# A hybrid encoder block: within-chunk products by array quadrants with compact operands, and two places for reloaded mixer outputs

## The chip, the cores and the metric

The kernel runs on one core of one Trainium2 chip. TensorE (PE) multiplies; VectorE (DVE), ScalarE (ACT) and GpSimd (POOL) do the rest; SyncE (SP) issues most of the transfers (DMA). The metric is the device time of one execution in microseconds (us), lower is better.

## The reference

One layer on 1024 tokens of width 1024: a projection, three parallel mixers (cross-attention to a memory, a Conformer convolution, a two-way RWKV-7 scan of 6 heads of 64), the output projection with its residual, then 16 experts that each pick 128 tokens. The part that the change touches is the scan and the output projection:

```python
def step(state, inp):
    r_t, w_t, k_t, v_t, kk_t, a_t = inp
    sa = jnp.einsum('bhij,bhj->bhi', state, -kk_t)
    state = (state * w_t[..., None, :]
             + sa[..., :, None] * (kk_t * a_t)[..., None, :]
             + v_t[..., :, None] * k_t[..., None, :])
    y_t = jnp.einsum('bhij,bhj->bhi', state, r_t)
    return state, y_t
...
x = x + jnp.concatenate([o_att, o_conv, o_rwkv], axis=-1) @ w_out[l]
x = x + expert_choice_ffn(rms_norm(x, norm_ffn_g[l]), w_router[l], w_e_gate[l], w_e_up[l], w_e_down[l])
```

## The kernel before

**Stages.** The projections, attention and convolution run first (to about 290 us of the trace), the scan follows (290 to about 750 us, overlapping the last projections at its start), then the rest of the output projection and the router, and from 890 us on the experts. Only the scan stage contains code that the change touches.

**The scan.** Sequences are cut into chunks of 64 tokens (`C`). Work is done in six units: three pairs of heads (one head on partitions 0 to 63, `lo`, the other on 64 to 127, `hi`) times two halves of the sequence; each unit holds 8 chunks (`HC`) for each of the two directions `d`. For one unit, `prep` builds two operands on DVE, ACT and POOL: `AR` (decayed kk and r, two blocks of 64 columns a chunk) and `BK` (k and b with the inverse decay, two blocks of 64). `within` multiplies them chunk by chunk into the within-chunk matrices; `prep2` transposes `BK` and v; `invert` solves a triangular system in 31 dependent steps on DVE (L910, L911); `chain` walks the 8 chunks one after the other, each a sequence of small products and copies: psX, Xs, psSA, SV, psS, S.

**The products of `within` before.** `BK` has room for both heads side by side, `[P, HC, 2, 2, C]`: the block that belongs to the other head is filled with zeros once (L668, L669), so that a product over all 128 partitions gives one head's result. A unit has four groups (a quarter of chunks `q`, a direction `d`), each with two tiles `psA`, one a head. A tile takes four matmuls of 128 rows by 128 columns with a moving operand of 128 columns, and is then multiplied by a mask into `AM` on DVE (L857). `psA` has two buffers in PSUM, so a tile is filled while the one before it is masked. ACT then copies parts of `AM` for `invert` (L895).

**The residual.** `residual` works off the first 5 of 8 row blocks of the output projection in 32 steps (4 column blocks of 256, 8 token blocks of 128). The mixer outputs were stored in DRAM as a high and a low part (`oT_d`) and are loaded back for each step as two tiles `fo`; 15 matmuls follow; DVE adds x (`fx`, L1089), and the sum goes to DRAM (L1090).

```python
1081                o = [Z["fw"].tile([P, 5, P], F32R, name=f"fo{j}", bufs=FOB) for j in range(2)]
1082                for j in range(2):
1083                    nc.sync.dma_start(o[j].bitcast(F32), oT_d[j][0:5, :, tok].rearrange("k p t -> p k t"))
1087                for k in range(5):
1088                    mm3(ps, o[0][:, k], o[1][:, k], wh[:, k], wl[:, k], k == 0, k == 4)
1089                V.tensor_add(xt, ps, xt)
```

With `FOB = 1` each of the two `fo` tiles has one place: the load of step i+1 must wait until the matmuls of step i have read it.

**What sets the order.** The stages are Python generators. `run` steps the `mains` in turn and puts steps of the `fills` (the next units' `prep`, `within`, `invert`, `prep2`, and the residual) between them by the numbers `R_*`. A scheduling layer then fixes the order on each engine; on the chip each engine, and SP's queue of transfers, works off its list in that order, and an instruction that waits holds up what stands behind it.

**Reading matmuls.** A matmul of 32-bit floats (`F32`) appears as two MATMUL records in the trace, so the eight matmuls of a pair of `psA` tiles are 16 records. Those of the residual and the projections are of another type (`F32R`) and appear as one.

Of the kernel before, what the change touches and what calls it, by code (L numbers as in the profile page):

```python
# [46 lines left out]
    _n += _w  # L47
NPC = _n

FOB = 1  # L50
RW = 1
LB = 1
KB = 2
# [47 lines left out]
def hybrid_block_kernel(ctx: ExitStack, tc: tile.TileContext, x, xT, memT, memn, w_in, w_mk, w_mv, pcols,  # L101
# [552 lines left out]
    def early():  # L654

        ph1r.close()
        Z["se"] = pool("se", bufs=2, stack=ph2r, side="right")
        Z["pcs"] = [Z["se"].tile([P, 2, HC], F32, name=f"pcs{i}", bufs=1) for i in range(3)]
        Z["s1"] = pool("s1", bufs=2, stack=ph2e, side="right")
        Z["ew"] = pool("ew", bufs=1, stack=ph2e, side="right")  # L660
        ge = pool("ge", stack=ph2e, side="right")
        Z["AR"] = [ge.tile([P, 2, HC, 2, C], F32, name="AR0")]
        Z["AM"] = [ge.tile([P, 4, 2, 2, C], F32, name=f"AM{i}") for i in range(4)]
        Z["TT"] = [ge.tile([P, NCH, 2, 32], F32, name="TT0")]

        Z["BK"] = [ge.tile([P, HC, 2, 2, C], F32, name=f"BK{d}") for d in range(2)]
        for bk in Z["BK"]:
            G.memset(bk[hi, :, 0], 0.0)  # L668
            G.memset(bk[lo, :, 1], 0.0)  # L669
        Z["ep"] = ge.tile([P, HC, C + 1], F32, name="ep")  # L670
        G.memset(Z["ep"][:, :, 0:1], 1.0)
        Z["dinit"] = dinit = ge.tile([P, 16, 32], F32, name="dinit")
        G.iota(dinit, pattern=[[-2, 16], [1, 32]], base=0, channel_multiplier=0,
               allow_small_or_imprecise_dtypes=True)
        V.tensor_scalar(dinit, dinit, lpar1, None, op0=ALU.is_equal)

        rst = ge.tile([P, HC, C], F32, name="rst")
        V.memset(rst, 1.0)
        V.memset(rst[:, :, 0:1], 0.0)
        Z["rst"] = rst.rearrange("p a b -> p (a b)")  # L680
        yield
# [93 lines left out]
    def prep(p, k, g):  # L775
        pd = pair[p]
        AR = g["AR"] = Z["AR"][g["u"] % 3]
        pcs = g["pcs"] = Z["pcs"][g["u"] % 3]
        if k == 0:
            pd["bonus"] = Z["se"].tile([P, NT, 2], F32, name="bonus", bufs=3)  # L780
            pd["prod"] = Z["s1"].tile([P, S], F32, name="prods", bufs=1)
        ins = [(load(f"k{p}", n), load(f"r{p}", n)) for n in (k, 1 - k)]
        for d in range(2):
            n = k if d == 0 else 1 - k
            rows = slice(d * 64, d * 64 + 64)
            kt, rt_ = ins[d]
            pw = mm()
            T.matmul(pw, lhsT=upw[rows, 0, p * P:(p + 1) * P], rhs=shifted["wd"][rows, half(k)], start=True, stop=True)
            pa = mm()
            T.matmul(pa, lhsT=upw[rows, 1, p * P:(p + 1) * P], rhs=shifted["ad"][rows, half(k)], start=True, stop=True)  # L790
            sg = Z["ew"].tile([P, HC, C], F32, name="sg", bufs=1)
            sg2 = sg.rearrange("p a b -> p (a b)")
            A.activation(sg2, pw, AF.Tanh, scale=0.5, bias=w0h[:, d * 3 + p:d * 3 + p + 1])
            ta = Z["ew"].tile([P, HC, C], F32, name="ta", bufs=1)
            A.activation(ta.rearrange("p a b -> p (a b)"), pa, AF.Tanh, scale=0.5,
                         bias=a0h[:, d * 3 + p:d * 3 + p + 1])
            yield
            if FL[0]:
                A.activation(sg2, sg2, AF.Identity, bias=1.0)
            else:  # L800
                V.tensor_scalar(sg, sg, 1.0, None, op0=ALU.add)
            cl = Z["ew"].tile([P, HC, C], F32, name="cl", bufs=1)
            V.tensor_tensor_scan(out=cl.rearrange("p a b -> p (a b)"), data0=Z["rst"], data1=sg2, initial=0.0,
                                 op0=ALU.mult, op1=ALU.add)
            ep = Z["ep"]
            A.activation(ep[:, :, 1:C + 1], cl, AF.Exp, scale=-0.5 * DECAY)

            A.activation(cl, cl, AF.Exp, scale=0.5 * DECAY)
            A.copy(pcs[:, d], ep[:, :, C])
            yield  # L810
            kk3, k3, r3 = chunks(pd["kk"][:, half(n)], d), chunks(kt, d), chunks(rt_, d)

            V.scalar_tensor_tensor(sg, ta, 1.0, kk3, op0=ALU.add, op1=ALU.mult)
            A.activation(ta, ta, AF.Identity, scale=kah[:, p:p + 1], bias=kac[:, p:p + 1])
            V.tensor_mul(AR[:, d, :, 0, :], kk3, ep[:, :, 0:C])
            yield
            (V, G)[FL[1]].tensor_mul(AR[:, d, :, 1, :], r3, ep[:, :, 1:C + 1])
            kd = ta
            (V, G)[FL[6]].tensor_mul(kd, k3, ta)
            yield  # L820

            BK = g["BK", d] = Z["BK"][d]
            V.tensor_mul(BK[lo, :, 0, 0, :], kd[lo], cl[lo])
            (G, V)[FL[7]].tensor_mul(BK[hi, :, 1, 1, :], kd[hi], cl[hi])
            for r_, h, i in ((lo, 0, 1), (hi, 1, 0)):
                V.scalar_tensor_tensor(BK[r_, :, h, i, :], sg[r_], -0.5, cl[r_], op0=ALU.mult, op1=ALU.mult)
            yield
            both = chunks(pd["prod"][:, half(n)], d)
            if k == 0:
                G.tensor_mul(both, kd, r3)  # L830
            else:
                prod = Z["ew"].tile([P, HC, C], F32, name="prod", bufs=1)
                G.tensor_mul(prod, kd, r3)
                G.tensor_add(both, both, prod)
            yield
        yield
# [8 lines left out]
    def within(g):  # L845

        for q, d in ((0, 0), (0, 1), (1, 0), (1, 1)):
            AM = g["AM", d, q] = Z["AM"][g["u"] % 2 * 4 + q * 2 + d]
            for h in range(2):
                ps = mm("A", shape=[P, 4, 2, C], name="psA", bufs=2)  # L850
                r_ = slice(h * 64, h * 64 + 64)
                for c in range(4):
                    cc = q * 4 + c
                    T.matmul(ps[:, c].rearrange("p a b -> p (a b)"),  # L854
                             lhsT=g["BK", d][:, cc, h].rearrange("p a b -> p (a b)"),
                             rhs=g["AR"][:, d, cc].rearrange("p a b -> p (a b)"), start=True, stop=True)
                V.tensor_tensor(AM[:, :, h], ps, mask[:, None].to_broadcast([P, 4, 2, C]), op=ALU.mult)  # L857
                yield

    def prep2(p, k, g):  # L860
        BT = g["BT"] = Z["BT"][g["u"] % 2]
        SV = g["SV"] = Z["SV"][g["u"] % 2]
        for d in range(2):
            n = k if d == 0 else 1 - k

            for h in range(2):
                ps = mm(shape=[P, HC, C])
                r_ = slice(h * 64, h * 64 + 64)
                for cc in range(HC):
                    T.transpose(ps[:, cc, :], g["BK", d][r_, cc, h].rearrange("p a b -> p (a b)"), ident[r_, r_])  # L870
                A.copy(BT[:, d, :, h, :], ps)
                yield

# [766 lines left out]
```

## Time and profile before

| | |
|---|---|
| three runs | 1480.89, 1490.68, 1491.66 us; median 1490.68 |
| the profiled execution | 1489.13 us, its span 1487.2 us |
| busy in the span | PE 90%, DVE 82%, ACT 56%, POOL 18% |
| granted clock of TensorE, mean of the span | 0.927 of 2.4 GHz |
| chain that ended last | PE 60%, DVE 23%, DMA 6%, ACT 5%, issue 4% |

Busy shares are averages over stages with different limits. The chain is followed back from the last instruction to whatever released each step; a time on it is a time on which the end depended in this execution. It does not tell how much slack the second-latest input had. Idle time in front of an instruction is given with what ended it.

### The profile page before, as it was taken

The page shows a single profiled execution, that of the slowest core. Times are in us where ns is not written, and L with a number is a line of the kernel's source. Part 1 is how long each engine was busy: PE and PEld are TensorE (multiplying, and loading weights), DVE is VectorE, ACT ScalarE, POOL GpSimd, SP SyncE. Part 2 cuts the span into 40 slices and gives each one's busy share as a digit, 9 for nine tenths or more (in the row PEclk, how much of TensorE's full clock was granted, in tenths as well). Part 3 has the DMA queues.
Part 4 walks back from the last instruction along what each step waited for, and adds up shares of the span by engine and source line. Part 5 has one row for each costly group of instructions (what it writes and reads, how often), then busy time and mean ns, then how long its engine had stood idle before and what let it go on. Part 6 is the DMA issues. An engine that isn't in the chain of part 4 may idle for free.

```text
span 1487.2 us, 24329 instructions
## 1 busy us (share of the span) xinstructions
PE 1333.4 (90%) x9238; PEld 1069.4 (72%) x9238; DVE 1216.1 (82%) x2120; ACT 831.2 (56%) x1214; POOL 266.4 (18%) x238
## 2 busy tenths in 40 slices
PE   6888999997888889888999719999999999999996
PEld 5777667675777776767868618888888887887773
DVE  8899975699686869696833678999999988998886
ACT  4222574433535244434322418888888877887875
POOL 2233322532120312130221000100000110110010
PEclk9999899998898888888999859999999999999998
DMA  8212112422443533342473657999999999999985
GB/s 294 71 61 67 64 64 97 152 71 73 141 143 93 157 97 117 105 121 84 142 272 142 269 198 293 386 393 390 385 385 390 381 379 344 370 377 377 370 302 201
DMA packets 146100, 327.91 MB, mean 220 GB/s; under 512 B 9792, under 2 KB 64960, under 8 KB 145984
## 3 DMA queue, kind: packets, MB, share of 16 engines
q1 hardware_dynamic: 139360, 303.14, 55.6%
q0 software_dynamic: 6192, 22.55, 5.4%
q8 instruction: 72, 1.18, 0.3%
q10 hardware_dynamic: 432, 0.68, 0.1%
q14 instruction: 44, 0.36, 0.1%
HBM read 288.58 MB, written 37.75 MB: 219 GB/s over the span
## 4 chain that ended last, share of the span: by engine, by line
PE 60%; DVE 23%; DMA 6%; ACT 5%; issue 4%; POOL 1%; SPq 0%; POOLq 0%; DVEq 0%; ACTq 0%
PE mm L330 14%; PE mm L331 14%; PE mm L329 14%; DVE cv L517 3%; DVE dtmp L910 2%; DVE Dt L911 2%; DMA fo<-oT_d 2%; PE mm L1435 2%; ACT Ld L895 2%; DMA xk<-in_xT_dram 1%; PE mm L745 1%; PE psA L854 1%; DVE ewl L1354 1%; PE mm L1165 1%; PE mm L1575 1%
## 5 line engine op out<-in xcount | busy, mean ns | idle before, releaser
L1354 DVE SCALAR_TENSOR_TENSOR ewl<-eraw,pc,ewh 128x1024 fp32r<-128x1024 f32 x256 | 315.6, 1280 | 30.5 <-ACT ewh L1353 28.4
L1353 ACT ACTIVATE ewh<-eraw,pc 128x1024 fp32r<-128x1024 f32 x256 | 283.8, 1149 | 31.7 <-PE mm L331 25.7
L330 PE MATMUL mm<-ewl,xh 128*128 128x512 f32 x512 | 202.1, 395 | 3.2 <-DVE ewl L1354 3.0
L331 PE MATMUL mm<-ewh,xl 128*128 128x512 f32 x512 | 200.1, 391 | 0.0
L329 PE MATMUL mm<-ewh,xh 128*128 128x512 f32 x512 | 190.4, 397 | 2.5 <-ACT ewh L1353 2.5
L1350 DVE TENSOR_TENSOR ewl<-eraw,ewh 128x1024 fp32r<-128x1024 f32 x120 | 139.0, 1219 | 2.8 <-ACT ewh L1349 2.8
L329 PE MATMUL mm<-hh,wh 128*128 128x512 f32 x304 | 125.4, 413 | 9.6 <-ACT hh L310 9.6
L1349 ACT ACTIVATE ewh<-eraw 128x1024 fp32r<-128x1024 f32 x120 | 121.6, 1057 | 10.6 <-PE mm L331 9.5
L331 PE MATMUL mm<-hh,wl 128*128 128x512 f32 x304 | 125.5, 413 | 0.8 <-POOL wl L325 0.8
L330 PE MATMUL mm<-hl,wh 128*128 128x512 f32 x304 | 125.1, 412 | 0.9 <-DVE hl L311 0.9
L330 PEld LDWEIGHTS mm<-ewl,xh 128*128 128x128 f32 x512 | 96.6, 189 | 25.8 <-DVE ewl L1354 7.3
L329 PEld LDWEIGHTS mm<-ewh,xh 128*128 128x128 f32 x512 | 96.1, 188 | 23.2 <-ACT ewh L1353 4.2
L331 PEld LDWEIGHTS mm<-ewh,xl 128*128 128x128 f32 x512 | 96.3, 188 | 19.7 <-DVE xl L1438 0.2
L330 PE MATMUL mm<-ewl,fh 128*128 128x512 f32 x240 | 94.6, 394 | 0.3 <-DVE ewl L1350 0.2
L331 PE MATMUL mm<-ewh,fl 128*128 128x512 f32 x240 | 93.6, 390 | 0.0
L329 PE MATMUL mm<-ewh,fh 128*128 128x512 f32 x240 | 88.0, 390 | 0.0
L325 POOL TENSOR_TENSOR wl<-wraw,wh 128x512 fp32r<-128x512 f32 x38 | 58.7, 1548 | 124.5 <-ACT wh L324 83.6
L329 PEld LDWEIGHTS mm<-hh,wh 128*128 128x128 f32 x304 | 59.6, 196 | 25.4 <-ACT hh L310 9.6
L1472 POOL DMA_INDIRECT x_d<-ye,idx x15 | 25.9, 1724 | 283.3 <-ACT ye L1471 283.3
L1420 POOL DMA_INDIRECT xe<-h_d,idx x16 | 28.9, 1805 | 247.0 <-DVE gates L1418 182.3
L517 DVE SCALAR_TENSOR_TENSOR cv<-u,cw,cv 128x512 f32<-128x512 f32 (+1 forms) x87 | 71.5, 853 | 0.1
L330 PEld LDWEIGHTS mm<-hl,wh 128*128 128x128 f32 x304 | 59.1, 194 | 17.4 <-issue 2.7
(417 smaller groups left out, 2950.7 us busy)
## 6 DMA issues: line engine op xcount, KB each, us to landing
eraw<-in_w_eg_dram SPq DMA_DIRECT2D x64, 1024.0 KB, 7.9
eraw<-in_w_eu_dram SPq DMA_DIRECT2D x64, 1024.0 KB, 9.1
eraw<-in_w_ed_dram SPq DMA_DIRECT2D x64, 1024.0 KB, 7.4
fo<-oT_d SPq DMA_DIRECT2D x64, 320.0 KB, 3.9
wraw<-in_w_in_dram SPq DMA_DIRECT2D x38, 256.0 KB, 2.8
ld_k<-d_k SPq DMA_DIRECT2D x18, 256.0 KB, 3.1
ld_v<-d_v SPq DMA_DIRECT2D x18, 256.0 KB, 3.3
xk<-in_xT_dram SPq DMA_DIRECT2D x16, 256.0 KB, 4.7
```

Of the source, the lines that this page charges most:

```text
L325: G.tensor_sub(wl, raw, wh.bitcast(F32))
L329: T.matmul(ps, lhsT=lh, rhs=rh, start=first, stop=False)
L330: T.matmul(ps, lhsT=lh, rhs=rl, start=False, stop=False)
L331: T.matmul(ps, lhsT=ll, rhs=rh, start=False, stop=last)
L517: V.scalar_tensor_tensor(o[:, 0:ln], z, w, o[:, 0:ln], op0=ALU.mult, op1=ALU.add)
L895: A.copy(Ld[r_, :, c:c + 4].rearrange("p t c -> p c t"), g["AM", d, q][r_, :, h, 0, b * 32:b * 32 + 32])
L910: IE.tensor_tensor(tmp[:, sg, ts], lcol, drow, op=ALU.mult)
L911: IE.tensor_tensor(Dt[:, sg, ts], Dt[:, sg, ts], tmp[:, sg, ts], op=ALU.add)
L1349: A.activation(h, raw[a], AF.Copy)
L1350: V.tensor_sub(l, raw[a], h.bitcast(F32))
L1353: A.activation(h, raw[a], AF.Copy, scale=gain)
L1354: V.scalar_tensor_tensor(l, raw[a], gain, h.bitcast(F32), op0=ALU.mult, op1=ALU.subtract)
```

## The change

Three edits. `BK` is compact, `[P, HC, 2, C]`: each head's partitions hold only its own k and b, in the block order that the transposes need; the four memsets are gone. `within` takes two PSUM tiles at once, one a head, and makes each chunk's product from four matmuls of 64 rows by 64 columns, one in each quadrant of the array: (partitions of the head) times (half of the result's partitions). `FOB` is 2: two places for each `fo` tile.

```diff
-FOB = 1
+FOB = 2
@@ early
-        Z["BK"] = [ge.tile([P, HC, 2, 2, C], F32, name=f"BK{d}") for d in range(2)]
-        for bk in Z["BK"]:
-            G.memset(bk[hi, :, 0], 0.0)
-            G.memset(bk[lo, :, 1], 0.0)
+        Z["BK"] = [ge.tile([P, HC, 2, C], F32, name=f"BK{d}") for d in range(2)]
@@ prep
-            V.tensor_mul(BK[lo, :, 0, 0, :], kd[lo], cl[lo])
-            (G, V)[FL[7]].tensor_mul(BK[hi, :, 1, 1, :], kd[hi], cl[hi])
-            for r_, h, i in ((lo, 0, 1), (hi, 1, 0)):
-                V.scalar_tensor_tensor(BK[r_, :, h, i, :], sg[r_], -0.5, cl[r_], op0=ALU.mult, op1=ALU.mult)
+            V.tensor_mul(BK[lo, :, 0, :], kd[lo], cl[lo])
+            (G, V)[FL[7]].tensor_mul(BK[hi, :, 1, :], kd[hi], cl[hi])
+            for r_, i in ((lo, 1), (hi, 0)):
+                V.scalar_tensor_tensor(BK[r_, :, i, :], sg[r_], -0.5, cl[r_], op0=ALU.mult, op1=ALU.mult)
@@ within
+            ps = [mm("A", shape=[P, 4, 2, C], name="psA", bufs=2) for _ in range(2)]
+            for c in range(4):
+                cc = q * 4 + c
+                for i, o in enumerate((lo, hi)):
+                    for h, r_ in enumerate((lo, hi)):
+                        T.matmul(ps[h][o, c].rearrange("p a b -> p (a b)"), lhsT=g["BK", d][r_, cc, i],
+                                 rhs=g["AR"][r_, d, cc].rearrange("p a b -> p (a b)"), start=True, stop=True)
             for h in range(2):
-                ps = mm("A", shape=[P, 4, 2, C], name="psA", bufs=2)
-                r_ = slice(h * 64, h * 64 + 64)
-                for c in range(4):
-                    cc = q * 4 + c
-                    T.matmul(ps[:, c].rearrange("p a b -> p (a b)"),
-                             lhsT=g["BK", d][:, cc, h].rearrange("p a b -> p (a b)"),
-                             rhs=g["AR"][:, d, cc].rearrange("p a b -> p (a b)"), start=True, stop=True)
-                V.tensor_tensor(AM[:, :, h], ps, mask[:, None].to_broadcast([P, 4, 2, C]), op=ALU.mult)
+                V.tensor_tensor(AM[:, :, h], ps[h], mask[:, None].to_broadcast([P, 4, 2, C]), op=ALU.mult)
                 yield
@@ prep2
-                    T.transpose(ps[:, cc, :], g["BK", d][r_, cc, h].rearrange("p a b -> p (a b)"), ident[r_, r_])
+                    T.transpose(ps[:, cc, :], g["BK", d][r_, cc].rearrange("p a b -> p (a b)"), ident[r_, r_])
```

The scheduling layer gives the engines of the scan stage another order. SP's queue near the start of the residual (fo: loads of steps; fx: loads of x; xacc_d: stores of sums; L1080, L1082 and L1087 of the changed kernel are L1083, L1085 and L1090 of before). Before:

```order
L1083 DMA fo_3372<-oT_d_134 128x5x128
L1090 DMA xacc_d<-fx 128x256
L1083 DMA fo_3373<-oT_d_135 128x5x128
L1085 DMA fx<-in_x_dram 128x256
L1083 DMA fo_3620<-oT_d_134 128x5x128
L1090 DMA xacc_d<-fx 128x256
L1083 DMA fo_3621<-oT_d_135 128x5x128
```

Of the change, at the same place:

```order
L1080 DMA fo_3680<-oT_d_134 128x5x128
L1080 DMA fo_3681<-oT_d_135 128x5x128
L1082 DMA fx<-in_x_dram 128x256
L1087 DMA xacc_d<-fx 128x256
L1080 DMA fo_3792<-oT_d_134 128x5x128
L1080 DMA fo_3793<-oT_d_135 128x5x128
```

Before, a step's loads stand just ahead of and behind the store of the step directly before them; now they stand ahead of that store, and the place that they fill was read one step earlier.

PE in unit 3, where a group of four psA products meets the chain (L966, L968, L973, L978) and the inversion (L931, L942; in the kernel before these are L969, L971, L976, L981, L934, L945). Before:

```order
L854 MATMUL psA<-AR_1934,BK_1940 128x128 x2
L1031 MATMUL mm<-y,bd_79 128x512
L854 MATMUL psA<-AR_1934,BK_1940 128x128 x2
L854 MATMUL psA<-AR_1934,BK_1941 128x128 x4
L753 MATMUL mm<-bd_75,ksq 128x2 x4
L981 MATMUL psSA<-Xs,TT_1939 64x64 x4
L854 MATMUL psA<-AR_1934,BK_1941 128x128 x4
```

Of the change, the same place:

```order
L851 MATMUL psA<-AR_1934,BK_1940 64x128 x2
L1028 MATMUL mm<-y,bd_79 128x512
L851 MATMUL psA<-AR_1934,BK_1940 64x128 x14
L749 MATMUL mm<-bd_75,ksq 128x2 x4
L978 MATMUL psSA<-Xs,TT_1939 64x64 x4
L749 MATMUL mm<-bd_75,gsq 128x2 x4
L851 MATMUL psA<-AR_1934,BK_1941 64x128 x16
```

A pair of tiles is now 16 small matmuls in one run instead of two runs of four, and the next pair stands further behind it.

PE at the end of unit 2's products in the changed kernel (the two groups of `BK_1940` and `BK_1941` are two pairs of tiles):

```order
L942 MATMUL mm<-TT_3035,W_4125 32x32 x32
L851 MATMUL psA<-ARb,BK_1940 64x128 x8
L851 MATMUL psA<-ARb,BK_1941 64x128 x16
L978 MATMUL psSA<-Xs,TT_3035 64x64 x4
```

Here a pair follows the one before it with nothing between.

## Rows read from the trace of the kernel before

**Rows 1.** Busy time by stretch: start:end, length, engines (records), granted clock, DMA.

```profile
core 0: us, PE busy (x) PEld busy (x) DVE busy (x) ACT busy (x) POOL busy (x), PEclk, DMA share, GB/s
365.00:745.00 380.00, 333.38 (x4214) 275.48 (x4214) 294.69 (x784) 153.37 (x312) 79.60 (x82) 0.84 0.40 121
290.00:365.00 75.00, 62.37 (x303) 48.72 (x302) 69.39 (x128) 29.24 (x49) 19.54 (x17) 0.95 0.16 56
```

**Rows 2.** The chain that ended last, 290 to 745 us, shares of that stretch.

```profile
by line: DVE dtmp L910 7.8%; DVE Dt L911 7.4%; DMA fo<-oT_d 6.0%; issue 5.7%; ACT Ld L895 5.6%; PE psA L854 4.1%; PE mm L329 3.6%; PE mm L331 3.5%; PE mm L330 2.8%; DVE BK L826 2.6%; PE mm L745 2.5%; DMA fraw<-in_w_out_dram 2.3%; DVE BK L82
```

**Rows 3.** Instructions of the tile fo: counts and times; idle before them; landing.

```profile
L1083 SPq DMA_DIRECT2D fo<-oT_d x64: 370/377/2688, 366.4 to 731.3; - x64
...
  DMA fo<-oT_d: 20.4, 23
...
DMA to landing us min/median/max: 3.1/3.9/5.9
```

**Rows 4.** Who waited for whom, 365 to 745 us: us, times, longest.

```profile
DVE fx L1089 <- PE mm L331: 20.5, 13, 4.4
...
DVE AM L857 <- PE psA L854: 6.0, 9, 1.5
...
PE mm L329 <- DMA fo<-oT_d: 5.3, 8, 1.6
PE mm L331 <- DMA fo<-oT_d: 4.9, 5, 1.7
```

**Rows 5.** Timeline of SP's queue, then PE, then DVE around one late load.

```profile
521.67 0.36 SPq L1090 DMA_DIRECT2D xacc_d<-fx  x1
522.13 0.38 SPq L1083 DMA_DIRECT2D fo<-oT_d  x1
...
528.12 0.39 PE L331 MATMUL mm<-fwh,fo 128*128 128x256 f32 x1 [1.75 <-DMA fo<-oT_d]
...
528.46 0.28 PE L330 MATMUL mm<-fwl,fo 128*128 128x256 f32 x1
528.58 0.28 PE L331 MATMUL mm<-fwh,fo 128*128 128x256 f32 x1
...
527.39 2.21 DVE L922 SCALAR_TENSOR_TENSOR TT<-Dr,pm,TT 128x512 f32<-128x512 f32 x2
```

**Rows 6.** Costliest groups, 290 to 760 us: busy us, mean ns of one | idle before.

```profile
L857 DVE TENSOR_TENSOR AM<-psA,mask 128x512 f32<-128x512 f32 x48 | 32.5, 684 | 7.4 <-PE psA L854 7.0
...
L854 PE MATMUL psA<-ARa,BK 128*128 128x128 f32 x128 | 22.4, 324 | 1.3 <-DVE AM L857 1.2
...
L854 PE MATMUL psA<-ARb,BK 128*128 128x128 f32 x128 | 21.0, 299 | 2.0 <-DVE BK L826 1.6 <-DVE Dt L911 0.4
...
L854 PE MATMUL psA<-AR,BK 128*128 128x128 f32 x128 | 19.4, 297 | 4.0 <-DVE BK L823 3.4 <-DVE AM L857 0.5
```

**Rows 7.** Timeline of PE: runs of matmuls of the whole array, and of two quadrants.

```profile
297.31 2.05 PE L854 MATMUL psA<-AR,BK 128*128 128x128 f32 x16 [1.41 <-DVE BK L823]
...
419.22 0.87 PE L882 MATMUL mm<-ident,ld_v 64*64 64x64 f32 x24
```

**Rows 8.** Timeline of PE: products of different quadrants beside each other.

```profile
402.49 0.28 PE L331 MATMUL mm<-fwh,fo 128*128 128x256 f32 x1
402.69 0.33 PE L971 MATMUL psX<-S,AR 64*64 64x64 f32 x4
402.86 0.23 PE L969 MATMUL psX<-SVa,AM 64*64 64x64 f32 x2
402.87 0.27 PE L976 MATMUL psY<-AR,S 64*64 64x64 f32 x2
402.92 0.23 PE L969 MATMUL psX<-SVa,AM 64*64 64x64 f32 x2
...
403.04 0.28 PE L976 MATMUL psY<-AR,S 64*64 64x64 f32 x3
```

**Rows 9.** Timeline of POOL: two of the four memsets.

```profile
272.01 0.94 POOL L668 MEMSET BK<- 64x1024 f32 x1
273.00 0.94 POOL L669 MEMSET BK<- 64x1024 f32 x1
```

## The prediction

> **What bounds the kernel now.** I looked first for the stretch in which the changed code runs, then for what the end depends on there. The table of stretches [rows 1] shows that until 365 us, where the last projections and the first unit overlap, DVE sets the pace: 69.4 of 75 us busy, against 62.4 for PE. From 365 to 745 us, where five of the six units and all 32 steps of the residual lie, neither engine does so alone: PE is busy 333 of 380 us (88%), DVE 295 (78%), and the granted clock of TensorE is 0.84 on average, so about a third of that stretch runs at 1.2 GHz instead of 2.4. Both engines work off fixed lists and wait for each other. The chain [rows 2] says the same in other words: the largest items of the 455 us from 290 to 745 us are DVE's inversion (7.8 and 7.4%), the loads of fo (6.0%, 27.3 us) and the products psA (4.1%, 18.7 us). Those two last items are the ones that the change reaches. After 745 us no changed instruction runs, and I take that part as it is.
>
> **The change, step by step.** The sum is made against the profiled execution, 1489.1 us (span 1487.2, 1.9 around it); it is 1.6 below the median of the three runs, which is nothing here.
>
> *The loads of fo.* There are 64 of them; a load lands 3.9 us after its issue in the median, 5.9 at most [rows 3]. One late load read closely [rows 5]: SP issues a step's second load at 522.13, behind the store of the step before; PE reaches the matmul that needs it and stands idle for 1.75 us until 528.12. In the new order of SP's queue the loads of a step stand ahead of the store of the step before, and wait only for matmuls two steps back. Steps come some 11.9 us apart (380 us for 32), so a load of 3.9 to 5.9 us has its time. I expect these waits to vanish almost entirely. What that is worth has two ends. PE's idle time in front of matmuls that waited for fo is 5.3 + 4.9 = 10.2 us [rows 4] (the 20.4 us of the tile's own view [rows 3] count weight loads as well). The chain has 27.3 us of these loads [rows 2], but that counts from the issue on, also while PE was at other work. Further, DVE sat 20.5 us before its additions `fx`, waiting for the residual's last matmul [rows 4]; part of that is the same lateness passed on. Against the full value speaks that in the wait of [rows 5] DVE was busy, with L922 from 527.39 on. I take 13 us, near the lower end, and keep 10 to 27.
>
> *The products psA.* Before, 16 records of the whole array take 2.05 us [rows 7]: less a tail of about 0.28 it is 0.118 us a record with 128 moving columns. In the change the same work is 32 records, each of a quarter of the array. What matters is whether the quadrants run beside each other. Two on the diagonal do: 24 records of L882 with 64 columns take 0.87 us [rows 7], less the tail 0.025 us each, where one at a time would be 0.059. Four do as well: L969 uses the two quadrants off the diagonal, L976 the two on it, and they start 0.01 us apart and go on beside each other [rows 8]. So a pair of tiles should take 32 / 4 = 8 rounds of 0.118, plus the tail: 1.22 us instead of 2.05, a share of 0.41 less. PE is busy with psA for 22.4 + 21.0 + 19.4 = 62.8 us over 24 pairs [rows 6], so PE is relieved of 25.4 us. On the path of this execution lie only 18.7 us of psA [rows 2], of which 0.41 is 7.6 us. I take 12, between the two and nearer the lower one, since DVE is nearly as busy as PE; I keep 7.6 to 25.4. DVE's own work stays: 48 maskings of 684 ns [rows 6].
>
> *The wait that is new.* Both PSUM tiles are now taken at once. The first matmuls of a pair need one tile of the pair before masked, the second matmul the other. So PE stands behind two maskings, 2 x 0.684 = 1.37 us, where before it filled one tile while the other was masked and waited 1.2 + 0.5 us in all [rows 6]. Behind the waiting matmul stands everything on PE, the chain's products included. Counted in the new order, three of the 24 pairs follow directly on another pair and eight more have three to ten matmuls between; the others have far more. At 1.4 us for the three and an estimated 0.7 for the eight this is 9.8 us of idle PE. DVE is busy in that time, with the very masks that ACT and the inversion wait for, so I put 4 us on the path; both ends are 0 and, if all 24 were uncovered and on the path, 33.
>
> *Switching.* Between matmuls of the whole array and of parts of it PE loses a little: from L331 to L971 it is 0.20 us from start to start [rows 8], against 0.12 between matmuls of the residual [rows 5], so about 0.09 a switch. Counted from the first psA to the last matmul of the residual, the order has 310 changes between kinds of matmul before and 320 now, since most small products now stand among the chain's, which are of the same kind. That is 1 us. [...]
>
> *The rest.* Four memsets of 0.94 us on POOL go [rows 9], at 272 us; PE is in the projections then and does not wait for POOL at that place, so 0 (3.8 us if it were the path). The writes of `BK` and its transposes keep their number and size: 0. The new order of DVE and ACT could cost or give some microseconds; I have no row for it and leave it to the range.
>
> **The sum.** -13 - 12 + 4 + 1 = -20 us: 1489.1 - 20 = 1469 us.
>
> **The rivals.**
>
> *PE alone sets the pace.* Then all of its relief counts: 25.4 of psA and the 10.2 of idle time before fo, 35.6 us: 1454 us. For it speaks PE's 88%, and that a higher clock could follow where PE waits less; against it DVE's 78% and the inversion at the top of the chain.
>
> *DVE and the clock swallow it.* PE finishes earlier and waits for DVE; lighter use of PE is followed by more time at 1.2 GHz, and what is left speeds up nothing. Then only what DVE itself waited for psA counts, 6.0 us [rows 4]: 1483 us, no change that can be told. For it speak DVE's busy time during the wait of [rows 5] and the 0.84 of [rows 1]; against it that DVE waits 20.5 us for the residual.
>
> *Slower, by the two tiles.* If the 24 pairs all wait for two maskings with the chain's products behind them, that is 33 us on the path; with 13 gained from fo and psA's gain lost in the wait, 1509 us. It decides from the point where the uncovered wait is over 25 us on the path; the order, with 13 of 24 pairs well apart, speaks against it.
>
> *The quadrants do not overlap.* Then a pair costs 32 x 0.118 + 0.28 = 4.06 us, PE has 2.0 x 24 = 48 us more, of which the share of psA on the chain (18.7 of 62.8) is 14; with 13 from fo the time is the old one, 1490 us. Against it speak [rows 8].
>
> **The numbers.** Chances: the forecast's case 0.50 (its own range 1458 to 1478), PE alone 0.15, swallowed 0.25, the two tiles 0.07, no overlap 0.03. A measurement of this kernel tells about 1% from no change, 14.9 us, so faster means below 1475.8 and slower above 1505.6. Faster: 0.9 of the forecast's case, 0.45, and PE alone 0.15, and a little of the swallowed case, 0.02: 0.62. Slower: the two tiles and 0.01 of the rest, 0.08. The same: 0.30. The range reaches from below PE alone, 1446 (a clock that rises with it), to above the swallowed case, 1490; what it leaves out is the slower case and most of the chain's full 27 us on top of everything.
>
> **What would show it.** In the profile of the change: 32 records of psA in about 1.2 us at full clock, in rows of 64*64; PE's busy time on psA near 37 us; idle time before matmuls on fo near nothing and fo gone from the chain; DVE's wait before `fx` below 20.5 us; PE's wait for masks (psA behind AM) about 10 us. Wrong would be the prediction if psA's rows stretch to 3 to 4 us, if the wait behind AM is over 25 us, or if the stretch from 290 to 745 us keeps its length with more idle time on PE or a clock below 0.84 there.

## The result, and the profile after

The change makes the kernel slower by three quarters of a per cent: 1499.18 us median of 20 runs (1488.25 to 1513.97), the kernel before 1487.26 us (1476.39 to 1498.66). The ratio is 1.0076, 95% interval 1.0054 to 1.0098, so +11 us where I had forecast -20. That is less than the 1% that the prediction named, but clear of the noise, outside the predicted range and on its other side. Ratios and clocks here and below leave out the few runs that lie over 1.5% above the fastest of their kernel (one of these 20).

The profiled execution of the change spans 1507.8 us, at a mean granted clock of 0.908 (0.927 before). First the table of stretches, as in [rows 1], and the chain, as in [rows 2]:

```profile
290.00:365.00 75.00, 68.91 (x380) 51.36 (x378) 64.02 (x126) 25.73 (x43) 20.17 (x16) 0.95 0.19 67
365.00:745.00 380.00, 327.35 (x4261) 261.03 (x4261) 289.24 (x744) 152.41 (x309) 75.56 (x79) 0.78 0.39 118
```

```profile
by line: DVE dtmp L907 9.1%; DVE Dt L908 6.8%; PE psA L851 6.2%; PE mm L329 5.1%; issue 4.7%; PE mm L330 4.4%; PE mm L331 4.3%; DVE BK L822 3.2%; PE psS L985 2.6%; DVE BK L819 2.4%; PE mm L784 2.2%; PE psSA L978 2.1%; ACT Ld L892 2.0%; PE m
```

From 365 to 745 us the clock is 0.78 instead of 0.84, and DVE is busy 5.5 us less: the stretch got less done. The loads of fo have left the chain's leading items: one piece of 3.3 us is left of them. psA has not: 6.2% instead of 4.1.

The view of the tile fo, as in [rows 3] (what its engine waited for, who waited for it, landing), and the costliest groups on psA, as in [rows 6], from 290 to 780 us:

```profile
its engine sat idle before it (us, times) until:
  DVE fwl L1074: 6.9, 6
...
  DVE fx L1086: 22.3, 13
...
DMA to landing us min/median/max: 3.2/4.0/6.8
```

```profile
L854 DVE TENSOR_TENSOR AM<-psA,mask 128x512 f32<-128x512 f32 x48 | 31.6, 681 | 14.9 <-PE psA L851 14.7
...
L851 PE MATMUL psA<-ARb,BK 64*64 64x128 f32 x256 | 24.1, 342 | 1.5 <-DVE BK L822 1.2 <-DVE AM L854 0.3
L851 PE MATMUL psA<-ARa,BK 64*64 64x128 f32 x256 | 21.5, 332 | 1.7 <-DVE BK L819 0.9 <-DVE rs_t L215 0.4 <-DVE AM L854 0.3
...
L851 PE MATMUL psA<-AR,BK 64*64 64x128 f32 x256 | 12.2, 298 | 4.5 <-DVE BK L819 4.5
```

The 20.4 us of idle time before fo are gone, though a load lands as late as before. But DVE waits for the residual as long as ever (22.3 us; 20.5 in [rows 4]), and twice as long for psA (14.7 us; 7.0 in [rows 6]). PE is busy with psA for 24.1 + 21.5 + 12.2 = 57.8 us, where I had expected 37. The timeline of PE tells why (start, duration, records, idle time before):

```profile
305.31 1.10 PE L851 MATMUL psA<-AR,BK 64*64 64x128 f32 x32 [1.41 <-DVE BK L819]
...
315.03 2.48 PE L851 MATMUL psA<-AR,BK 64*64 64x128 f32 x32 [3.04 <-DVE BK L819]
```

```profile
392.65 1.97 PE L851 MATMUL psA<-ARa,BK 64*64 64x128 f32 x16 [0.95 <-DVE BK L819]
394.91 1.54 PE L851 MATMUL psA<-ARa,BK 64*64 64x128 f32 x10 [0.29 <-DVE AM L854]
```

At full clock (1.00 from 305.3 to 306.4 us) the four quadrants do run beside each other: 32 records in 1.10 us. But the same 32 take 2.48 us at 315, at half clock (0.50 from 315.0 to 317.5) and behind 3.04 us of idle time, and at 392, at 0.50 as well, a run of 16 takes 1.97. Where the clock stood, in stretches of 8 us (columns as in [rows 1]), first before, then after:

```profile
312.00:320.00 8.00, 8.00 (x45) 6.86 (x45) 6.07 (x15) 4.17 (x10) 1.50 (x2) 1.00 0.24 94
...
384.00:392.00 8.00, 7.67 (x170) 7.32 (x171) 2.76 (x7) 4.95 (x9) 0.00 (x0) 1.00 0.29 89
392.00:400.00 8.00, 6.40 (x63) 5.56 (x62) 5.45 (x18) 6.38 (x17) 0.00 (x0) 0.94 0.43 131
400.00:408.00 8.00, 6.83 (x84) 6.04 (x84) 5.65 (x26) 0.93 (x3) 0.80 (x2) 0.85 0.40 110
```

```profile
312.00:320.00 8.00, 4.97 (x38) 4.18 (x39) 7.90 (x7) 1.44 (x3) 6.05 (x3) 0.63 0.25 73
...
384.00:392.00 8.00, 5.47 (x86) 4.91 (x84) 5.66 (x9) 5.16 (x11) 4.04 (x3) 0.50 1.01 313
392.00:400.00 8.00, 7.07 (x98) 6.30 (x98) 3.81 (x7) 1.64 (x3) 1.93 (x1) 0.50 0.34 112
400.00:408.00 8.00, 8.00 (x107) 7.20 (x104) 1.05 (x3) 5.84 (x11) 0.00 (x0) 0.50 0.06 18
```

From 384 to 408 us the clock of PE is 0.50 after the change and 0.85 to 1.00 before; the change is some 11 us behind by then, so the same work stands one or two lines further down, at 0.50 for the most part. Starts of the same DVE instruction in both traces put the loss there: the change is 8.0 us behind at 281 us of the kernel before, 10.7 at 382, about 20 at 450, and 20.6 at the end. Of these, some 6.5 us arise near 130 us, ahead of every changed instruction; most profiled executions below don't show them. Without them the loss is 14 us, close to the +12 of the medians, and nearly all of it arises between 281 and 450 us. So the theories to tell apart were: the clock falls because the products use less of the array; the two tiles at once delay the masks; the second place for fo brings a worse order.

### The profile page after: what moved, and what is told of

It reads as the page before. It is cut to its first block, busy times and chain, and to the rows that moved or that the text cites. A ratio compares the mean times of both kernels' runs of the same rounds, so it can differ in the third digit from the quotient of the medians.

```text
span 1507.8 us, 25121 instructions
## 1 busy us (share of the span) xinstructions
PE 1348.5 (89%) x9622; PEld 1069.2 (71%) x9622; DVE 1214.4 (81%) x2120; ACT 831.1 (55%) x1214; POOL 268.7 (18%) x234
## 4 chain that ended last, share of the span: by engine, by line
PE 62%; DVE 24%; DMA 5%; issue 4%; ACT 3%; POOL 2%; SPq 0%; POOLq 0%; DVEq 0%; ACTq 0%
PE mm L330 14%; PE mm L329 14%; PE mm L331 14%; DVE cv L517 3%; DVE dtmp L907 3%; DVE Dt L908 2%; PE psA L851 2%; PE mm L1432 2%; DVE ewl L1351 1%; PE mm L1162 1%; PE psS L985 1%; DVE BK L822 1%; PE mm L1572 1%; PE mm L1413 1%; PE mm L608 1%
## 5 line engine op out<-in xcount | busy, mean ns | idle before, releaser
L325 POOL TENSOR_TENSOR wl<-wraw,wh 128x512 fp32r<-128x512 f32 x38 | 66.9, 1764 | 128.2 <-ACT wh L324 110.6
L331 PEld LDWEIGHTS mm<-hh,wl 128*128 128x128 f32 x304 | 60.4, 199 | 21.4 <-POOL wl L325 7.9
L907 DVE TENSOR_TENSOR dtmp<-Lt,Dt 128x126 f32<-128x126 f32 (+22 forms) x186 | 73.1, 393 | 2.7
```

The lines of the kernel that those rows point to most:

```text
L325: G.tensor_sub(wl, raw, wh.bitcast(F32))
L331: T.matmul(ps, lhsT=ll, rhs=rh, start=False, stop=last)
L907: IE.tensor_tensor(tmp[:, sg, ts], lcol, drow, op=ALU.mult)
```

## The experiments

All ratios are against the kernel before, run beside each kernel on the same chip. The clock is the median over each kernel's runs of the mean granted clock; "lost" is (1 - clock) times the span, an accounting figure: the time at full clock that the throttle took, on the path or not. The kernel before has a clock of 0.926 and loses 110 us; the change has 0.912 and loses 132.

| run | ratio (95%) | clock | lost us |
|---|---|---|---|
| compact_fob1: compact, one tile at a time, 64 rows | 1.0130 (1.0071 to 1.0190) | 0.901 | 150 |
| full_fob1: the same over 128 rows | 1.0002 (0.9975 to 1.0029) | 0.926 | 110 |
| compact_fob2 | 1.0173 (1.0104 to 1.0241) | 0.905 | 144 |
| full_fob2 | 1.0019 (0.9988 to 1.0050) | 0.927 | 109 |
| rows_fob2: two tiles at once, two row halves | 1.0107 (1.0073 to 1.0141) | 0.904 | 144 |
| quad_fob1: the change with FOB = 1 | 1.0123 (1.0070 to 1.0175) | 0.907 | 141 |
| full_two: two tiles at once, 128 rows, FOB = 1 | 1.0069 (1.0033 to 1.0106) | 0.924 | 114 |
| rows_twice | 1.0253 (1.0204 to 1.0302) | 0.914 | 131 |
| quad_twice | 1.0160 (1.0116 to 1.0205) | 0.918 | 124 |
| up_compact: compact_fob1, full-row up-projections | 1.0103 (1.0060 to 1.0145) | 0.913 | 131 |
| up_after: the change, full-row up-projections | 1.0012 (0.9978 to 1.0045) | 0.924 | 113 |
| tr_after: the change, merged transposes | 1.0070 (1.0039 to 1.0102) | 0.916 | 126 |
| uptr_after: both | 1.0038 (1.0009 to 1.0066) | 0.922 | 117 |
| up_before2: the kernel before, full-row up-projections | 0.9963 (0.9933 to 0.9992) | 0.938 | 93 |
| up_full: full_fob1, full-row up-projections | 0.9975 (0.9947 to 1.0003) | 0.935 | 96 |
| inv_less: before, 8 of 31 inversion steps left out | 0.9865 (0.9826 to 0.9903) | 0.936 | 95 |

### Rows of the array: compact_fob1 and full_fob1

`compact_fob1` has the compact operand and nothing else of the change; TensorE's order is nearly that of the kernel before.

```diff
-                             lhsT=g["BK", d][:, cc, h].rearrange("p a b -> p (a b)"),
-                             rhs=g["AR"][:, d, cc].rearrange("p a b -> p (a b)"), start=True, stop=True)
+                             lhsT=g["BK", d][r_, cc].rearrange("p a b -> p (a b)"),
+                             rhs=g["AR"][r_, d, cc].rearrange("p a b -> p (a b)"), start=True, stop=True)
```

> Compact BK alone, one tile at a time and FOB = 1: TensorE's order is that of the kernel before, row for row; only the four memsets on GpSimd are gone and a product reads 64 rows instead of 128. Every theory expects 0.998 to 1.002. If halves of the array run beside each other across the two tiles, psA's busy time falls from 62.8 us; one tile of four products takes 1.0 us at full clock if they don't.

It is 1.3% slower, which no theory had expected. `full_fob1` puts `:` back in place of `r_` in both operands.

> Compact BK, one tile at a time, FOB = 1, as in the run compact_fob1, but each product contracts over all 128 rows: it adds the two heads up, which is not the wanted sum, and the mask is scaled by 0.01 so that the numbers stay small. TensorE's order is that of compact_fob1 but for a few rows. If the loss of compact_fob1 (1.013, mean granted clock 0.90) comes from half of the array's rows lying idle in psA: 0.997 to 1.003, clock 0.92. If it comes from anything else in the compact operand (its place, the missing memsets): 1.013 again, clock 0.90.

The loss is gone, and with it the loss of clock. The two kernels have nearly the same order on TensorE and differ in whether a product of psA uses 64 or 128 of the array's rows; beside that, the values of `AM`, and of what is worked out from it, differ (sums of two heads, scaled by 0.01). That other values give the clock back can be left aside: the kernel before has the same values as compact_fob1, all rows in use, and a clock of 0.926. In stretches of 8 us, full_fob1 and then compact_fob1:

```profile
304.00:312.00 8.00, 6.04 (x35) 4.93 (x34) 7.94 (x10) 4.22 (x9) 4.43 (x3) 1.00 0.18 61
312.00:320.00 8.00, 7.46 (x49) 6.44 (x48) 6.18 (x11) 4.94 (x12) 2.21 (x2) 1.00 0.38 133
320.00:328.00 8.00, 8.00 (x36) 6.44 (x35) 7.67 (x21) 2.42 (x3) 1.67 (x2) 1.00 0.11 34
...
392.00:400.00 8.00, 8.00 (x125) 7.48 (x123) 3.93 (x12) 7.64 (x17) 0.00 (x0) 1.00 0.40 114
```

```profile
304.00:312.00 8.00, 5.81 (x31) 4.76 (x29) 7.94 (x10) 3.96 (x9) 4.69 (x3) 0.89 0.14 49
312.00:320.00 8.00, 8.00 (x34) 6.15 (x34) 4.01 (x8) 3.27 (x8) 1.96 (x2) 0.50 0.37 133
320.00:328.00 8.00, 8.00 (x33) 6.46 (x32) 5.38 (x10) 2.98 (x6) 0.95 (x1) 0.75 0.00 0
...
392.00:400.00 8.00, 7.86 (x93) 7.29 (x93) 2.69 (x7) 2.97 (x6) 0.00 (x0) 0.51 0.23 68
```

What PE did just before, in the same order of kernels:

```profile
309.88 2.02 PE L850 MATMUL psA<-AR,BK 128*128 128x128 f32 x16 [1.96 <-DVE BK L819]
```

```profile
309.62 2.58 PE L850 MATMUL psA<-AR,BK 64*128 64x128 f32 x16 [2.19 <-DVE BK L819]
```

Both had waited about 2 us for DVE and then went on with psA. Behind that the clock falls in compact_fob1 (0.50 from 312 to 320 us) and not in full_fob1 (1.00), and this although PE is busy 8.00 of these 8 us in compact_fob1 and 7.46 in full_fob1. Whether the other 64 rows hold zeros (the kernel before) or another head (full_fob1) makes no difference that can be measured: 1.0002, and a clock of 0.926 in both. So the busy time of PE does not by itself tell its clock in these two runs; the rows in use differ, and the clock with them.

### The second place for fo: full_fob2, compact_fob2, quad_fob1

Each differs from its partner in `FOB` alone.

> The same with FOB = 2: the second place for fo with all rows of the array in use (sums of both heads, mask scaled by 0.01). If the second place gains what the idle time before fo was worth: 0.991 to 0.996. If its order of the residual costs more than that: 1.003 to 1.010; compact_fob2 against compact_fob1 was 1.004.

> FOB = 2 with the compact BK, but one psA tile at a time: four products of 64 rows by 128 columns to a tile, as many and as long as before. If FOB and its order cause the loss: 1.005 to 1.010. If the loss lies in the products: 0.990 to 0.996, that is the 10 us of idle PE before fo gained; the predicted 13 us would be 0.991.

> The changed kernel with FOB back at 1: quadrant products and the two-tile step alone. If the products (order, two-tile wait, clock) cause the loss of 0.8%, this is slower than the kernel before by at least that, 1.008 to 1.015, since the 10 us of idle PE before fo are back as well. If the second place for fo and the order that follows from it cause the loss, this is at 0.993 to 1.000 of the kernel before.

The idle time before fo, in the tile view (us, times), in full_fob1 and in full_fob2:

```profile
  DMA fo<-oT_d: 18.9, 22
```

```profile
  DMA fo<-oT_d: 2.7, 5
```

The wait goes as predicted, 16 us of it, and the time does not follow: 1.0019 against 1.0002. The other two pairs read +0.4% (compact_fob2 against compact_fob1) and -0.5% (the change against quad_fob1), each within its intervals. No gain from the second place can be measured. The expectation of 0.991 to 0.996 was a miss; so was the other theory, that its order costs 0.3 to 1%. quad_fob1 is slower than the kernel before by 1.2% without it, so the change's loss lies in the products; compact_fob2 lies above both expectations because it has the idle rows of compact_fob1 as well.

### Two tiles at once, and halves beside each other: rows_fob2, full_two

`rows_fob2` keeps the two tiles of the change, with eight products of 64 rows by 128 columns in place of sixteen quadrants. `full_two` takes the two tiles at once with full_fob1's products.

```diff
             ps = [mm("A", shape=[P, 4, 2, C], name="psA", bufs=2) for _ in range(2)]
             for c in range(4):
                 cc = q * 4 + c
+                for h, r_ in enumerate((lo, hi)):
+                    T.matmul(ps[h][:, c].rearrange("p a b -> p (a b)"),
+                             lhsT=g["BK", d][r_, cc].rearrange("p a b -> p (a b)"),
+                             rhs=g["AR"][r_, d, cc].rearrange("p a b -> p (a b)"), start=True, stop=True)
```

> Both tiles at once and FOB = 2 as in the change, but eight products of 64 rows by 128 columns for a pair, one half of the rows beside the other, instead of sixteen in quadrants. If the two-tile step causes the loss, as slow as the change: 1.005 to 1.010. If the number of small instructions, or the order that the scheduling layer gives to sixteen, causes it: 0.990 to 1.000. A pair of tiles should take about 1.2 us at full clock here too.

> full_fob1 with both psA tiles taken at once and filled in turn, each product over all 128 rows (the two heads added up, mask scaled by 0.01): the two-tile step of the change without its quadrants, at the clock of before. The prediction's price of the new wait was 4 us, 1.003; if the coupling of the two tiles costs more, 1.006 to 1.015; if it costs nothing, 0.998 to 1.002.

Row halves run beside each other too; timeline of PE in rows_fob2, a pair of tiles at full clock (matmuls of 512 columns behind it start 0.23 us apart) and one at half (0.43 us apart):

```profile
300.49 1.16 PE L850 MATMUL psA<-AR,BK 64*128 64x128 f32 x16 [1.40 <-DVE BK L819]
...
313.56 2.67 PE L850 MATMUL psA<-AR,BK 64*128 64x128 f32 x16
```

rows_fob2 reads 0.7% faster than compact_fob2, at the same clock; that is within the noise of the pair, so a gain from less work of TensorE on psA is not shown. It is not faster than the change, so the number of small instructions is not the cause. full_two is 0.7% (10 us) slower than full_fob1, clear of the noise, at nearly the same mean clock: taking two tiles at once has a price. It is not the wait that I had priced. In both traces PE's idle time before psA that ended with a mask is 2.0 us. In the profiled pair most of the difference (some 7 of 9 us) arises in one step, between 465 and 490 us. Stretches of full_fob1, then of full_two:

```profile
468.00:476.00 8.00, 7.88 (x73) 5.47 (x72) 4.38 (x12) 6.37 (x16) 0.55 (x1) 0.91 0.32 94
476.00:484.00 8.00, 7.45 (x107) 6.09 (x101) 7.12 (x23) 3.33 (x8) 0.87 (x1) 1.00 0.17 48
484.00:492.00 8.00, 6.10 (x86) 5.26 (x85) 7.75 (x14) 1.48 (x4) 4.95 (x5) 0.87 0.68 207
```

```profile
468.00:476.00 8.00, 5.09 (x47) 4.19 (x46) 3.50 (x9) 5.97 (x16) 0.06 (x1) 0.89 0.08 25
476.00:484.00 8.00, 8.00 (x47) 4.19 (x47) 4.37 (x13) 2.74 (x6) 0.34 (x1) 0.50 0.39 115
484.00:492.00 8.00, 8.00 (x66) 6.63 (x64) 3.06 (x12) 1.22 (x3) 1.06 (x1) 0.50 0.02 5
```

In full_two PE waits there for copies of DVE and ACT (1.26 and 1.65 us), and behind that it has a clock of 0.50 from 476 to 492 us. So in this pair the step goes with a fall of the clock behind waits that the other order brings. In the medians the throttle takes only 4 us more (114 and 110), so whether the 10 us arise this way in the other runs is open.

### More work for the clock: rows_twice, quad_twice

Every product of psA is made twice, so that TensorE should be as long at it as before the change (62.8 us); it came out longer, 88.8 and 81.2 us.

> As the run rows_fob2 (both row halves beside each other, FOB = 2), but every product of psA is made twice, the second over the first: TensorE is as long busy with psA as in the kernel before, 2.05 us a pair, with all rows in use. If the clock follows how much of the array works: mean clock from 0.904 back to about 0.92, ratio 0.997 to 1.005, no slower than rows_fob2 in spite of 25 us more of TensorE's work. If the clock has no part in it: 1.015 to 1.028, slower than rows_fob2 by 8 to 25 us.

> The changed kernel with every quadrant product made twice. As for rows_twice: by the clock 0.995 to 1.006, no slower than the change; if the clock has no part in it, 1.012 to 1.025.

The clock rises in both, from 0.904 to 0.914 and from 0.912 to 0.918, and still both are slower than their partners, by 1.5 and 0.8%. In rows_twice psA keeps PE busy for 88.8 us from 290 to 790 us, in rows_fob2 for 59.3: 29.5 us more work cost 22 us. Buying clock with work does not pay here, and the times came out on the side of the theory without the clock. These two runs change work and clock together, and with them the order, so they don't tell the theories apart; the next ones change rows and little else.

### Filling idle rows elsewhere: the runs with up-projections and transposes

The products L788 and L790 in `prep` use 64 rows as well: a direction's low-rank input times the weights of the decay (L788) or of `a` (L790), 512 moving columns. With the other direction's rows zero in a padded copy of the weights, the same products run over 128 rows:

```diff
-            T.matmul(pw, lhsT=upw[rows, 0, p * P:(p + 1) * P], rhs=shifted["wd"][rows, half(k)], start=True, stop=True)
+            T.matmul(pw, lhsT=Z["upw"][:, d, 0], rhs=shifted["wd"][:, half(k)], start=True, stop=True)
```

The diff is that of `up_before2`, which has one small tile that GpSimd's queue reloads for each pair of heads. In the other runs, kernels with the compact operand, all padded weights are resident (`Z["upw"][:, d, 0, p * P:(p + 1) * P]`).

> compact_fob1 (1.013) with the up-projections of prep, the products of 64 rows by 128 columns with 512 moving columns, made over all 128 rows: the weights of the two directions stand in a padded tile, the other direction's rows zero. No product gets longer or shorter. If idle rows cost the clock, idle rows that are filled elsewhere give it back: these products are about 31 us of TensorE's time against 63 of psA, so half of the loss, 1.004 to 1.009, with the mean clock up from 0.901 to about 0.912. If psA's rows matter for another reason: 1.011 to 1.016.

> The change (1.0076) with the same full-row up-projections. By idle rows: 0.997 to 1.003, clock from 0.912 to about 0.92. Otherwise 1.006 to 1.010.

> full_fob1 (1.0002: psA over all rows with the two heads added up, mask scaled by 0.01) with the full-row up-projections as in up_compact, all weights resident. By idle rows and clock: 0.992 to 0.998, clock above 0.926. Otherwise 0.999 to 1.003.

> The kernel before with the up-projections of prep over all 128 rows; the padded weights of a pair of heads stand in one small tile that GpSimd's queue reloads at the start of each pair. If idle rows lower the clock here too: 0.992 to 0.998, with the mean clock above 0.926. If rows matter only in psA, or the reloads come late: 0.999 to 1.006.

up_after takes the change from 1.0076 back to 1.0012, clear of the noise. up_before2 makes the kernel before faster: 0.9963, interval below 1, the only version here that beats both and leaves nothing out. up_full goes the same way (0.9975), within the noise. up_compact reads 0.3% faster than compact_fob1 at 0.012 more clock, less than expected and within the noise. The groups of these products before and in up_before2 show that they did not get longer, though padded:

```profile
L790 PE MATMUL mm<-s_ad,upw 64*128 64x512 f32 x23 | 16.0, 778 | 1.8 <-ACT SVa L884 1.8
...
L788 PE MATMUL mm<-s_wd,upw 64*128 64x512 f32 x22 | 14.7, 753 | 0.0
```

```profile
L791 PE MATMUL mm<-s_wd,upw 128*128 128x512 f32 x24 | 15.1, 717 | 0.0
...
L793 PE MATMUL mm<-s_ad,upw 128*128 128x512 f32 x24 | 14.6, 692 | 1.5 <-ACT SVa L887 1.5
```

The same for the transposes of `BK`, which the compact operand allows to be merged, one of 128 by 128 for both heads instead of two of 64 rows:

```diff
-                    T.transpose(ps[:, cc, :], g["BK", d][r_, cc].rearrange("p a b -> p (a b)"), ident[r_, r_])
+                    T.transpose(ps[:, c, :], g["BK", d][:, q * 4 + c].rearrange("p a b -> p (a b)"), ident)
```

> The change with the transposes of BK merged: one of 128 by 128 a chunk for both heads, which the compact operand allows, instead of two of 64 rows. TensorE's time on them stays about the same (21 us) or falls, all rows are in use. By idle rows: 1.000 to 1.005. Otherwise 1.006 to 1.010, or a little less if the transposes themselves get shorter.

> The change with both, the full-row up-projections and the merged transposes. By idle rows: 0.990 to 0.998, clock 0.92 or above, faster than the kernel before since TensorE has less work at the same clock. Otherwise 1.005 to 1.010.

These two missed. tr_after is no faster than the change (1.0070), and its clock rose only from 0.912 to 0.916. uptr_after is not faster than up_after, nor than the kernel before, though its clock from 290 to 790 us is nearly that of the kernel before and PE is busy 12 us less. The same stretch of before, of uptr_after and of up_before2:

```profile
290.00:790.00 500.00, 437.76 (x5070) 356.28 (x5070) 379.88 (x957) 194.08 (x381) 110.63 (x110) 0.87 0.38 121
```

```profile
290.00:790.00 500.00, 425.54 (x5328) 329.76 (x5327) 377.92 (x954) 194.76 (x382) 107.36 (x109) 0.86 0.39 121
```

```profile
290.00:790.00 500.00, 433.03 (x5092) 350.07 (x5092) 380.54 (x960) 194.97 (x384) 114.22 (x114) 0.89 0.39 123
```

Why full-row transposes bring nothing where full-row products do is open.

### VectorE's part: inv_less

> The kernel before without 8 of the 31 steps of the inversion (j = 10 to 17, so the inverse is not the wanted one): 35.4 us less of VectorE's work, nothing else. If VectorE's inversion sets the pace of the scan, so that a lighter TensorE gains nothing: 0.977 to 0.988. If TensorE sets it: 0.995 to 1.001, or slower where its clock falls.

The time falls by 20 us (14 to 26). Busy time in the whole trace, from the pages of before and of inv_less:

```profile
PE 1333.4 (90%) x9238; PEld 1069.4 (72%) x9238; DVE 1216.1 (82%) x2120; ACT 831.2 (56%) x1214; POOL 266.4 (18%) x238
```

```profile
PE 1323.4 (90%) x9238; PEld 1059.8 (72%) x9238; DVE 1185.2 (81%) x2024; ACT 831.6 (57%) x1214; POOL 270.8 (18%) x238
```

DVE is busy 30.9 us less, not 35.4. Compare a stretch of inv_less with that of before above: PE is busy 12.4 us more, so it waits less, and it has a higher clock.

```profile
290.00:790.00 500.00, 450.13 (x5241) 364.43 (x5240) 359.32 (x879) 200.94 (x393) 116.97 (x111) 0.91 0.40 129
```

So DVE's inversion lies on the path of the scan: two thirds of what it is relieved of come back as time, at the edge of what was expected if it sets the pace. How much of that is DVE's own pace and how much the clock, this run does not separate: the throttle takes 95 us instead of 110. That a lighter load on PE alone pays little is what uptr_after shows.

## Why the prediction was wrong

Step by step, in microseconds; 1% is 14.9. The right column is made of differences between runs, each uncertain by 4 to 13 us; only the idle rows and the two tiles are clear of that.

| step | predicted | the runs |
|---|---|---|
| loads of fo | -13 | +6 (compact_fob2 less compact_fob1); +2 and -7 in the two other pairs |
| psA's products shorter | -12 | -10 for halves beside each other, the price of two tiles included (rows_fob2 less compact_fob2), -5 for quadrants in place of halves |
| two tiles at once | +4 | contained in the -10; by itself +10 at full rows (full_two less full_fob1) |
| switching | +1 | not measured |
| memsets and writes of `BK` | 0 | 0 (full_fob1, 1.0002) |
| half of the rows idle | not in the sum | +19 (compact_fob1 less full_fob1) |
| sum | -20 | +11, as measured |

The runs of the right column form a chain from the kernel before to the change (full_fob1, compact_fob1, compact_fob2, rows_fob2), so that its sum must meet the measured time and is no test of the steps.

**The step that failed: the clock was taken as given.** I priced psA's products at the clock of the kernel before and put the clock only into a rival, in which it could swallow the gain down to the 6 us that DVE itself waited (1483 us). It can do more than swallow: the runs show 19 us for idle rows alone (9 to 29), one tile at a time and with TensorE's order nearly unchanged. What the rival assumed, "lighter use of PE is followed by more time at 1.2 GHz", is what the runs with shorter or compact products of psA show (clock 0.912 in the change, 0.901 in compact_fob1, 0.926 before); its bound was wrong. With what I read as waste in the kernel before, half of every psA product multiplied with zeros, the clock is 0.926; with the same products over 64 rows, in compact_fob1, it is 0.901. The change takes the zeros away for all 24 pairs: the time that the throttle takes rises from 110 to 132 us, and the span less that time falls from 1376 to 1366. By this account 10 us are gained and 22 of clock lost. Two pairs bear on the change itself. quad_fob1 against full_two has the two tiles at once and one place for fo in both, and differs in quadrants against full rows: its clock is 0.907 against 0.924, and it reads 8 us slower (uncertain by 10) although PE has less to do. up_after has full rows elsewhere: the clock of the change goes from 0.912 to 0.924 and 10 us come back; but the same edit gives the kernel before 6 us, so it does not show that the loss is the clock's alone. How much of the 22 us comes of rows that lie idle and how much of PE being done sooner with psA and then waiting, no run separates.

**The loads of fo.** This term failed too. The idle time before fo and its place in the chain went, as predicted [rows 2, 3]; the 13 us did not follow, nor the low end of 10. That end was PE's idle time [rows 4]; but PE's idle time is only worth something where PE is what the others wait for. I had listed as a gain to come that DVE waits for the residual less; it waits 22.3 us instead of 20.5. That DVE was busy during the wait of [rows 5] was the better sign.

**psA.** A pair takes 1.10 us at full clock (predicted 1.22), from [rows 7] and [rows 8]; that quadrants don't overlap is refuted. PE's busy time on it fell from 62.8 to 57.8 us and not to 37: a pair at a clock of 0.50 takes 2.48 us, and many runs are broken up, such as that at 392.65, whose products start two at a time. So PE was relieved of 5 us instead of 25, and no run shows a gain from it that is clear of the noise.

**Two tiles.** The wait behind masks that I counted out at 9.8 us is 2.5 in the view of the tile psA of the change (its engine sat idle before it, us, times):

```profile
  DVE AM L854: 2.5, 7
```

The step still costs 10 us at full rows, in another way than I had written: in the profiled pair most of it goes with a fall of the clock. The rival of 1509 us, all pairs waiting, did not happen.

**What would show it.** Three of the signs held: 1.1 us a pair at full clock, no idle time before fo, fo all but gone from the chain. Three did not: psA at 37 us (57.8), DVE's wait before `fx` below 20.5 (22.3), about 10 us of waiting behind masks (2.5). Of those that would show me wrong, the last came true: a stretch that does not get shorter, at a clock below 0.84 (0.78).

Open remain: why the transposes behave otherwise, whether two tiles cost their 10 us by the clock in every run, and what the columns of the array, as against its rows, do to the clock; no run had idle columns alone.

## What to carry to other kernels

Before taking zero padding out of a matmul whose stretch shows a granted clock below 1, price the clock: compare the work taken out with the time that the throttle takes now, and try the full-row form first. Here PE's time on psA fell by 5 us, and the time that the throttle takes rose by 22. Look for products of 64 rows among heavy ones; filling their idle rows with zeros cost no TensorE time here and was worth 0.4% (0.1 to 0.7, up_before2). Before pricing an idle gap of one engine in front of a load, look in the trace for who waits for that engine meanwhile: here 16 us of such a gap went (full_fob2 against full_fob1), and no gain can be measured.

## What the runs showed of the hardware

- A stretch in which PE is busy 8.00 of 8 us can have a clock of 0.50: compact_fob1 from 312 to 320 us, behind a wait of 2.19 us, while full_fob1, with nearly the same order and a wait of 1.96, has 1.00. Rows filled with zeros gave the same clock here as rows filled with data: full_fob1, whose rows all hold data, is at 1.0002 of the kernel before, in which half hold zeros, and both have a clock of 0.926.
- In the traces of before and of the change the clock is 0.50 or 1.00 at any moment; values between are means over a stretch. In the change, matmuls of 512 moving columns start 0.427 us apart at 0.50 (318.0 to 319.7 us) and 0.234 at 1.00 (309.0 to 311.4). 512 columns in 0.427 us are 1.2 a nanosecond: from this the 1.2 GHz of the prediction, and 2.4 for twice that, can be had as an estimate, if a column takes a cycle.
- 32-bit products of 64 by 64 in the four quadrants start so close together that 32 records with 128 moving columns take 1.10 us at a clock of 1.00; two row halves, 16 records, 1.16 us; the whole array one by one, 16 records, 2.05 [rows 7].
- Not every run in quadrants has all four at work: at 392.65, at a clock of 0.50, 16 records start two at a time, 0.21 us apart, and take 1.97 us, where at 315.03, at 0.50 too, 32 in one run take 2.48. In the run at 305.31, at 1.00, they start four at a time, 0.11 us apart.
